# A third buffer for the adaLN filler's weight tiles, each asked for two steps ahead, in a two-layer hybrid diffusion step

## The chip, the core and the metric

The kernel runs on one core of one Trainium2 chip, as one program. The metric is the device time of one execution in microseconds; of several runs the median counts. Engines are named as in the profile: PE (TensorE, matrix products; its weight loads are PEld), DVE (VectorE), ACT (ScalarE), POOL (GpSimd) and SP (SyncE, which here does nothing but issue DMAs). Each engine works through its own list of instructions in the order in which it stands there; semaphores make one engine wait for another or for a DMA.

## The reference, cut to what matters

Two layers (`DEPTH = 2`, `D_MODEL = 2048`) over 128 context tokens and 512 latent tokens, in float32. In each layer a condition vector, one for the context tokens (`c_ctx`) and one for the latent ones (`c`), gives shift, scale and gate:

```python
def adaln(cvec, w, b):
    m = jax.nn.silu(cvec) @ w + b          # w: 2048 x 6144 per layer
    return jnp.split(m, 3, axis=-1)

def layer_step(x, cvec, p, rope, attend, s0_f, s0_b):
    ...
    shift, scale, gate = adaln(cvec, w_ada, b_ada)
    h = rms_norm(x, norm_g) * (1.0 + scale) + shift
    aq, ak, av, ag, bq, bff, bfb, bi, bg, cu, cv, cg = split_proj(h @ w_in)
    ...                                    # windowed attention, HGRN2 recurrence, gated MLP
    y = jnp.concatenate([a_out, b_out, c_out], axis=-1) @ w_out
    return x + gate * y, k, v, s_f, s_b
```

Latent attention works in blocks of 128 queries; a query sees the keys at most 128 positions away and all 128 cached context keys. So the block before and the block after need a triangular mask each, and the others none.

## The kernel before, in words

The 640 tokens stand on five tiles of 128 (`NT = 5`). The normed input is kept transposed, as 16 pairs (`KT = 16`, one per 128 input features) of tiles `hh` and `hl`, a float32 split in two parts for PE. Weights come from HBM as raw tiles `wr` (128x512, 256 KB), and are split by ACT into `wh` and by DVE into `wl`. A product is three matmuls: `hh` with `wh`, `hh` with `wl`, `hl` with `wh` (lines 682 to 684 with tokens on the output's partitions, 15 matmuls of 512 columns for each of the 16 `k`; line 690 the other way round). Four `wr` and three `wh`/`wl` buffers let loads and splits run ahead.

Layer 0 begins with `first_round`. It needs the scale of layer 0 before it can make any `hh`/`hl`, and gets it in six chunks of 2 or 4 `k`: for a chunk it loads that part of `w_ada` (raw tiles, also called `wa` in the profile, or `mg` where they are large), multiplies it on PE (line 249) with the condition vectors, which stand padded in the tile `pad`, and DVE writes the result to `gs` (lines 296 and 297). Then `scaled_h` makes `hh` on ACT (line 396) and `hl` on DVE (line 397) for each `k` of the chunk, and PE multiplies them with the key and value columns and with the first 128 columns of `cu`. The matmuls of one chunk run while the next chunk's scale is computed. x comes in six loads (`const_xT`), the weights of this round as `wr` or `ev`. `second_round` (query columns) gets the shift in the same way, and `bias_rows` multiplies it, in a second `pad` tile, with the weights already used and adds it to what was computed; only then are both `pad` tiles free.

The other columns of `w_ada` (gate of layer 0; shift, scale and gate of layer 1) aren't needed soon. They are the **filler**: `ada_gen` yields step by step through 16 blocks of 512 columns, and `fill()`, called after each weight group of the main path, takes 0.85, 0.5 or 1.25 steps on the average. A step loads one tile `wa` of 128x512 (256 KB, line 305) and DVE adds it, times a scalar, to the accumulator `aacc`, once for each condition vector (line 309 for the first tile of a block, line 311 for the 15 others). At a block's end PE sums `aacc` over its partitions (lines 317 and 328). There is one `aacc`, so a block's first step waits for the end of the block before. The filler's tiles come from the pool `arp`, which has two buffers; the two `pad` tiles come from the same pool.

All this is written in one order, and a scheduler then sets the order of each engine's list, by priorities, its own estimate of times and the buffers that are free. What is written under `hi()` goes ahead of the rest: the loads of weights and of the filler's tiles, and the whole start of layer 0. At most eight DMAs that SP issued are in flight: each takes one of eight semaphores in turn and waits until the DMA that had it has landed.

Of the kernel before, what the change touches and what calls it, by code (L numbers as in the profile page):

```python
# [18 lines left out]
P = 128  # L19
# [23 lines left out]
def host_consts():  # L43
    c = {}
    grid_w, theta, hd, n = 64, 10000.0, 128, 512
    row = np.repeat(np.arange(n // grid_w), grid_w).astype(np.float32)
    col = np.tile(np.arange(grid_w), n // grid_w).astype(np.float32)
    half = hd // 2
    freq = (np.float32(theta) ** (-np.arange(0, half, 2, dtype=np.float32) / np.float32(half))).astype(np.float32)
    ang = np.stack([row[:, None] * freq, col[:, None] * freq], axis=1).astype(np.float32)  # L50
    cs, sn = np.cos(ang), np.sin(ang)
    c["rope"] = np.ascontiguousarray(
        np.stack([cs, sn]).reshape(2, 4, P, hd // 2).transpose(2, 0, 1, 3)
    ).astype(np.float32)
    q = np.arange(P)[:, None]
    k = np.arange(P)[None, :]
    prev = np.where(k >= q, 0.0, NEG).astype(np.float32)
    nxt = np.where(k <= q, 0.0, NEG).astype(np.float32)
    z = np.zeros((P, P), np.float32)
    c["mask"] = np.concatenate([prev, z, nxt, z, prev, z, z, nxt], axis=1)  # L60
    misc = np.zeros((P, 256), np.float32)
    misc[:, 0:128] = np.eye(P)
    misc[:, 192:217] = 1.0
    misc[:, 192:217:5] = 0.0
    dneg = np.zeros((5, 4), np.float32)
    for i in range(4):
        dneg[i, i + 1:] = NEG
    misc[:, 224:244] = dneg.reshape(-1)
    for cd in range(2):
        misc[cd::32, 248 + cd] = 1.0  # L70
    c["misc"] = misc
    c["tri"] = np.stack([q <= k, q >= k], axis=1).astype(np.float32)
    return c


class Net:
# [7 lines left out]
    def pools(self):  # L84
        tc, ctx = self.tc, self.ctx
        ec = ctx.enter_context
        self.cst = ec(tc.tile_pool(name="cst", bufs=1))
        self.sml = ec(tc.tile_pool(name="sml", bufs=3))
        self.hp = ec(tc.tile_pool(name="hp", bufs=KT))
        self.mgp = ec(tc.tile_pool(name="mgp", bufs=5))  # L90
        self.wrp = ec(tc.tile_pool(name="wrp", bufs=4))
        self.whp = ec(tc.tile_pool(name="whp", bufs=3))
        self.arp = ec(tc.tile_pool(name="arp", bufs=2))
        self.evp = ec(tc.tile_pool(name="evp", bufs=5))
        self.gp = ec(tc.tile_pool(name="gp", bufs=7))
        self.pm = ec(tc.tile_pool(name="pm", bufs=5, space=PSUM))
        self.psd = ec(tc.tile_pool(name="psd", bufs=3, space=PSUM))
        self.dr = ec(tc.tile_pool(name="dr", bufs=1, space=DRAM))
# [35 lines left out]
    def setup(self):  # L134
        nc, I, C = self.nc, self.I, self.C
        cst = self.cst
        nc.scalar.preload_act_table_set("natural_log_exp_and_others")
        CR = self.g(128)
        nc.sync.dma_start(CR[0:16], I["c_ctx"].rearrange("(a p) -> a p", p=P))
        nc.sync.dma_start(CR[16:32], I["c"][0].rearrange("(a p) -> a p", p=P))  # L140
        misc = cst.tile([P, 256], F32, name="misc")
        nc.scalar.dma_start(misc, C["misc"])
        self.ident = misc[:, 0:128]
        self.m25 = misc[:, 192:217]
        self.dneg = misc[:, 224:244]
# [34 lines left out]
    def setup2(self):  # L180
        nc, I, C = self.nc, self.I, self.C
        cst = self.cst
        R = self.g(128)
        nc.scalar.dma_start(R[0:32], I["b_ada"][1, 0:4096].rearrange("(a p) -> a p", p=P))
        nc.scalar.dma_start(R[32:48], I["hgrn_lb"].rearrange("l d (h p) -> (l d h) p", p=P))
        nc.scalar.dma_start(R[48:50], I["hgrn_norm_g"])
        b = self.bank()
        nc.tensor.transpose(b[:, 0:50], R[0:50, :], self.ident[0:50, 0:50])
        nc.vector.tensor_copy(self.cols[:, 64:114], b[:, 0:50])
        l0, l1 = self.cols[:, 96:104], self.cols[:, 104:112]  # L190
        lt = self.g(64).rearrange("p (a b) -> p a b", a=8)
        mx, e0, e1, sm_, p0, p1 = (lt[:, i] for i in range(6))
        nc.vector.tensor_tensor(mx, l0, l1, op=ALU.max)
        nc.vector.tensor_tensor(e0, l0, mx, op=ALU.subtract)
        nc.vector.tensor_tensor(e1, l1, mx, op=ALU.subtract)
        nc.scalar.activation(lt[:, 1:3], lt[:, 1:3], AF.Exp)
        nc.vector.tensor_tensor(sm_, e0, e1, op=ALU.add)
        nc.vector.reciprocal(sm_, sm_)
        nc.vector.tensor_tensor(p0, e0, sm_, op=ALU.mult)
        nc.vector.tensor_tensor(p1, e1, sm_, op=ALU.mult)  # L200
        self.lb = cst.tile([P, 2, 8], F32, name="lb")
        self.oml = cst.tile([P, 2, 8], F32, name="oml")
        nc.vector.tensor_tensor(self.lb[:, 0], p0, p0, op=ALU.subtract)
        nc.vector.tensor_tensor(self.lb[:, 1], p0, p1, op=ALU.add)
        nc.vector.tensor_tensor(self.lb[:, 1], self.lb[:, 1], p0, op=ALU.subtract)
        nc.vector.tensor_scalar(self.oml, self.lb, -1.0, 1.0, op0=ALU.mult, op1=ALU.add)
        self.rope = cst.tile([P, 2, 4, 64], F32, name="rope")
        nc.scalar.dma_start(self.rope, C["rope"])
        self.scan_f = cst.tile([P, T], BF16, name="scan")
        nc.vector.memset(self.scan_f, 1.0)  # L210
        nc.vector.memset(self.scan_f[:, 0:T:32], 0.0)
        self.m8 = cst.tile([P, 2, P], U8, name="m8")
        mf = self.g(256)
        nc.scalar.dma_start(mf, C["tri"].rearrange("p d k -> p (d k)"))
        nc.vector.tensor_copy(self.m8.rearrange("p d k -> p (d k)"), mf)
        self.mask = cst.tile([P, 8 * P], BF16, name="mask")
        for i in range(2):
            mf = self.g(512)
            nc.scalar.dma_start(mf, C["mask"][:, 512 * i:512 * i + 512])
            nc.vector.tensor_copy(self.mask[:, 512 * i:512 * i + 512], mf)  # L220
        self.att = [cst.tile([P, P], F32, name=f"att{d}") for d in range(2)]
        self.tp = [cst.tile([P, 5, 5], F32, name=f"tp{i}") for i in range(2)]
        for d in range(2):
            nc.gpsimd.memset(self.tp[d], 0.0)
            nc.gpsimd.memset(self.att[d], 0.0)
        self.snk = cst.tile([P, 2, 8], F32, name="snk")
        self.nsnk = cst.tile([P, 2, 8], F32, name="nsnk")
        nc.scalar.dma_start(self.snk, I["attn_sink"].partition_broadcast(P))
        nc.vector.tensor_scalar(self.nsnk, self.snk, -1.0, None, op0=ALU.mult)
        self.gd = [self.dr.tile([2, D], F32, name=f"gd{l}", tag=f"gd{l}") for l in range(DEPTH)]  # L230
        self.cud = [self.dr.tile([P, T], F32, name=f"cud{h}", tag=f"cud{h}") for h in range(4)]
        self.x1 = [self.dr.tile([P, D], F32, name=f"x1_{t}", tag=f"x1_{t}") for t in range(NT)]
# [63 lines left out]
            nc.vector.scalar_tensor_tensor(gs, ps, 1.0, col(48 + 32 * l), op0=ALU.add, op1=ALU.add)  # L296
            nc.vector.tensor_tensor(gs, gs, col(16 * l), op=ALU.mult)

    def ada_steps(self, l, blk):
        nc = self.nc  # L300
        acc = self.sml.tile([P, 2, 512], F32, tag="aacc", name=self.nm("aacc"), bufs=1)
        for k in range(KT):
            with self.hi():
                r = self.arp.tile([P, 512], F32, tag="ar", name=self.nm("wa"))
                nc.sync.dma_start(r, self.I["w_ada"][l, k * P:(k + 1) * P, 512 * blk:512 * blk + 512])
            for cd in range(2):
                sc = self.s2[:, k, cd:cd + 1]
                if k == 0:
# [22 lines left out]
        yield  # L331

    def ada_gen(self, items):
        for it in items:
            yield from self.ada_steps(*it)

    def fill(self):
        self.credit += self.fill_rate
# [371 lines left out]
    def colmajor(self, W, c0):  # L710
        ps = [self.mbank() for _ in range(2)]
        for k4 in range(0, KT, 4):
# [7 lines left out]


    KPOS = {1: 3, 2: 4, 3: 0, 4: 1}
    WIN = {1: (((2, 1, 3),), 5, (0, 1, 2)),
# [3 lines left out]

    def kblk(self, gi, part):
        return self.kT[:, gi, part]
# [165 lines left out]
    def attn(self, l, gi, t):  # L895
# [11 lines left out]
        if t > 0:  # L907
# [9 lines left out]
            for h in range(4):  # L917
# [1 line left out]
                hs = slice(h * P, h * P + P)  # L919
                o = 0  # L920
                for p0, ds, pn in pieces:
                    ks = slice(p0, p0 + ds * pn, ds)
                    so = s[:, o * P:(o + pn) * P].rearrange("p (b k) -> p b k", k=P)
                    for i, (x, y) in enumerate(((qh, kh), (qh, kl), (ql, kh))):
                        nc.tensor.matmul(so, lhsT=x[:, hs], rhs=y[:, ks], start=i == 0, stop=i == 2,  # L925
# [525 lines left out]
```

## Time and profile before

| what | value |
|---|---|
| median of 3 runs | 2282.91 us (2281.86 to 2283.32) |
| profiled execution, its own time | 2287.63 us |
| its span, first to last instruction | 2285.8 us |
| PE busy | 2242.6 us, 98% |
| DVE busy | 1381.1 us, 60% |
| ACT busy | 943.9 us, 41% |
| DMA | 299.03 MB, mean 131 GB/s |

The first two lines differ by 4.7 us: the profiled execution is a run of its own. Its time is 1.8 us longer than the span of its instructions. In the profile's rows, `out<-in` names what an instruction writes and reads, without buffer numbers; x and a number is a count; in a timeline the first number is the start in us, the second the busy time, and the bracket at the end the engine's idle time just before, with what ended it. PE's records overlap, since its ends are modelled: the distance from start to start is what a matmul really takes. A `q` behind an engine's name means its sequencer, which issues the DMA.

### The profile page before, as it was taken

What the parts mean: (1) busy time and instruction counts of PE and PEld (TensorE: products, weight loads), DVE (VectorE), ACT (ScalarE), POOL (GpSimd) and SP (SyncE); (2) the same over time, 40 slices, a digit from 0 to 9 for tenths busy, and PEclk for the clock granted to TensorE, in tenths of its full rate; (3) what the DMA queues carried; (4) which work ended last, traced back from release to release, by engine and by line L of the source; (5) the groups of instructions that cost most, each with busy time, mean ns of one, the idle gap of its engine ahead of it and who ended that gap; (6) DMA issues with size and microseconds to landing.
All of it is one profiled execution on the core that took longest, in us unless ns stands there. A gap on an engine that the chain in (4) does not pass through costs nothing.

```text
span 2285.8 us, 35095 instructions
## 1 busy us (share of the span) xinstructions
PE 2242.6 (98%) x13259; PEld 1945.6 (85%) x13259; DVE 1381.1 (60%) x2666; ACT 943.9 (41%) x2306; POOL 0.7 (0%) x8
## 2 busy tenths in 40 slices
PE   7999999999999999999989999999999999999999
PEld 4766778999999998978877887799999999898887
DVE  4457967748577575776668555844846644264332
ACT  3423355445464562422223345543635545233111
POOL 0000000000000000000000000000000000000000
PEclk9999999999999999999999999999999999999999
DMA  9776533324334254465553321422423322326332
GB/s 354 243 258 209 171 95 117 117 78 145 103 114 133 83 154 129 144 224 182 177 181 94 101 61 48 131 60 82 140 76 103 111 69 82 94 70 205 113 106 79
DMA packets 265550, 299.03 MB, mean 131 GB/s; under 512 B 16771, under 2 KB 166165, under 8 KB 263845
## 3 DMA queue, kind: packets, MB, share of 16 engines
q1 hardware_dynamic: 252656, 270.09, 37.9%
q10 hardware_dynamic: 12724, 26.71, 3.7%
q8 instruction: 104, 1.70, 0.3%
q14 instruction: 66, 0.53, 0.1%
HBM read 281.69 MB, written 15.04 MB: 130 GB/s over the span
## 4 chain that ended last, share of the span: by engine, by line
PE 87%; DVE 6%; DMA 5%; ACT 1%; issue 1%; ACTq 0%; SPq 0%; DVEq 0%
PE m L690 36%; PE m L682 12%; PE m L684 12%; PE m L683 12%; DMA wa<-in_w_ada_dram 4%; DVE aacc L311 2%; PE s L249 2%; PE s L925 2%; PE s L971 1%; PE s L1138 1%; DVE wl L671 1%; PE s L983 1%; PE s L690 1%; PE s L984 1%; PE s L1153 1%
## 5 line engine op out<-in xcount | busy, mean ns | idle before, releaser
L671 DVE TENSOR_TENSOR wl<-wr,wh 128x512 fp32r<-128x512 f32 (+1 forms) x535 | 366.5, 687 | 547.5 <-ACT wh L670 546.5
L670 ACT ACTIVATE wh<-wr 128x512 fp32r<-128x512 f32 (+1 forms) x535 | 335.9, 629 | 870.6 <-PE m L684 501.7
L683 PE MATMUL m<-wl,hh 128*128 128x512 f32 x1440 | 568.1, 395 | 5.9 <-DVE wl L671 5.7
L682 PE MATMUL m<-wh,hh 128*128 128x512 f32 x1440 | 571.0, 397 | 1.6 <-ACT hh L396 1.5
L684 PE MATMUL m<-wh,hl 128*128 128x512 f32 x1440 | 566.1, 393 | 0.0
L690 PE MATMUL m<-hh,wh 128*128 128x384 f32 x2016 | 479.1, 317 | 0.2 <-DVE ev L1189 0.2
L690 PE MATMUL m<-hh,wl 128*128 128x384 f32 x2016 | 468.1, 311 | 0.0
L690 PE MATMUL m<-hl,wh 128*128 128x384 f32 x2016 | 467.3, 311 | 0.0
L311 DVE SCALAR_TENSOR_TENSOR aacc<-wa,s,aacc 128x512 f32<-128x512 f32 x480 | 344.1, 746 | 84.9 <-DMA wa<-in_w_ada_dram 82.7
L682 PEld LDWEIGHTS m<-wh,hh 128*128 128x128 f32 x1440 | 271.9, 189 | 73.8 <-issue 9.8
L683 PEld LDWEIGHTS m<-wl,hh 128*128 128x128 f32 x1440 | 272.0, 189 | 65.7 <-DVE wl L671 9.6
L690 PEld LDWEIGHTS m<-hh,wh 128*128 128x128 f32 x2016 | 310.8, 189 | 14.7 <-issue 9.3
L684 PEld LDWEIGHTS m<-wh,hl 128*128 128x128 f32 x1440 | 271.8, 189 | 58.5 <-issue 2.4
L690 PEld LDWEIGHTS m<-hh,wl 128*128 128x128 f32 x2016 | 311.5, 189 | 2.0 <-issue 1.8
L690 PEld LDWEIGHTS m<-hl,wh 128*128 128x128 f32 x2016 | 311.2, 189 | 2.0 <-issue 1.4
L1124 ACT ACTIVATE mg<-ev,Dt 128x32 f32<-128x32 f32 x480 | 113.3, 309 | 10.3 <-PE s L1138 10.1
L955 ACT ACTIVATE g<-g,st,qs 128x384 f32<-128x384 f32 (+1 forms) x64 | 48.1, 752 | 31.6 <-DVE st L951 31.6
L975 DVE TENSOR_TENSOR g<-s,g 128x512 fp32r<-128x512 f32 x56 | 38.6, 690 | 36.3 <-ACT g L974 29.2
L971 PE MATMUL s<-misc,g 128*128 128x128 f32 x240 | 45.6, 284 | 5.9 <-ACT g L960 5.1
L960 ACT ACTIVATE g<-g,st 128x384 f32<-128x384 f32 (+2 forms) x80 | 43.9, 605 | 13.3 <-DVE st L958 13.3
L925 PE MATMUL s<-kT,g 128*128 128x256 f32 (+1 forms) x288 | 47.3, 305 | 0.0
L971 PEld LDWEIGHTS s<-misc,g 128*128 128x128 f32 x240 | 29.6, 142 | 20.1 <-ACT g L960 12.3
(278 smaller groups left out, 1832.4 us busy)
## 6 DMA issues: line engine op xcount, KB each, us to landing
wr<-in_w_in_dram SPq DMA_DIRECT2D x406, 256.0 KB, 2.9
wa<-in_w_ada_dram SPq DMA_DIRECT2D x296, 256.0 KB, 2.9
wr<-in_w_out_dram SPq DMA_DIRECT2D x128, 256.0 KB, 3.0
wa<-in_w_ada_dram SPq DMA_DIRECT2D x16, 1024.0 KB, 7.0
wa<-in_w_in_dram SPq DMA_DIRECT2D x9, 1024.0 KB, 6.4
mg<-in_w_ada_dram SPq DMA_DIRECT2D x4, 1280.0 KB
x<-mg SPq DMA_DIRECT2D x20, 256.0 KB, 2.6
mg<-x ACTq DMA_DIRECT2D x5, 1024.0 KB, 6.1
```

The source lines that it names most:

```text
L249: return self.nc.tensor.matmul(acc[32 * q:32 * q + 32, 0:n], lhsT=lhs[:, kk, :], rhs=rhs, start=kk < 4, stop=kk >= 12, skip_group_check=True)
L311: nc.vector.scalar_tensor_tensor(acc[:, cd], r, sc, acc[:, cd], op0=ALU.mult, op1=ALU.add)
L670: nc.scalar.activation(wh, raw, AF.Copy)
L671: nc.vector.tensor_tensor(wl, raw, wh.bitcast(F32), op=ALU.subtract)
L682: nc.tensor.matmul(ps, lhsT=hh, rhs=wh[:, 0], start=k == 0, stop=False)
L683: nc.tensor.matmul(ps, lhsT=hh, rhs=wl[:, 0], start=False, stop=False)
L684: nc.tensor.matmul(ps, lhsT=hl, rhs=wh[:, 0], start=False, stop=k == KT - 1)
L690: self.nc.tensor.matmul(ps[hf][:, 0:n], lhsT=w[:, a], rhs=h[:, o:o + n], start=k == 0 and i == 0, stop=k == KT - 1 and i == 2)
L925: nc.tensor.matmul(so, lhsT=x[:, hs], rhs=y[:, ks], start=i == 0, stop=i == 2, skip_group_check=True)
L955: nc.scalar.activation(dst[h], src[h], AF.Exp, bias=nmx[:, h:h + 1], scale=rq[:, h:h + 1], accum_out=den[:, h:h + 1])
L971: nc.tensor.transpose(pb[:, h * P:(h + 1) * P], dst[h][:, kb * P:(kb + 1) * P], self.ident)
L1124: nc.scalar.activation(blk[:, 4 * i + q], e[:, q], AF.Copy, scale=dd[:, i, c:c + 1])
```

## The change

Three things. The pool `arp` gets a third buffer. The load of a filler tile goes into a function of its own, `ada_load`, which takes the next tile from a list that runs over all blocks; `ada_gen` calls it twice before the first step, and each step calls it once more before it takes its own tile from the front of the queue `ahead`. To make room in SBUF, the mask tile shrinks from eight blocks of 128 columns to four, and a constant tile from 256 columns to 192; the table `WIN`, which says for each query block which key blocks are read in which order and where its mask begins, changes with it.

```diff
-    c["mask"] = np.concatenate([prev, z, nxt, z, prev, z, z, nxt], axis=1)
-    misc = np.zeros((P, 256), np.float32)
+    c["mask"] = np.concatenate([prev, z, z, nxt], axis=1)
+    misc = np.zeros((P, 192), np.float32)
...
-        self.arp = ec(tc.tile_pool(name="arp", bufs=2))
+        self.arp = ec(tc.tile_pool(name="arp", bufs=3))
...
-        self.mask = cst.tile([P, 8 * P], BF16, name="mask")
-        for i in range(2):
-            mf = self.g(512)
-            nc.scalar.dma_start(mf, C["mask"][:, 512 * i:512 * i + 512])
-            nc.vector.tensor_copy(self.mask[:, 512 * i:512 * i + 512], mf)
+        self.mask = cst.tile([P, 4 * P], BF16, name="mask")
+        mf = self.g(512)
+        nc.scalar.dma_start(mf, C["mask"])
+        nc.vector.tensor_copy(self.mask, mf)
...
-    def ada_steps(self, l, blk):
+    def ada_load(self, tiles):
+
+        at = next(tiles, None)
+        if at is None:
+            return
+        l, blk, k = at
+        with self.hi():
+            r = self.arp.tile([P, 512], F32, tag="ar", name=self.nm("wa"))
+            self.nc.sync.dma_start(r, self.I["w_ada"][l, k * P:(k + 1) * P, 512 * blk:512 * blk + 512])
+        self.ahead.append(r)
+
+    def ada_steps(self, l, blk, tiles):
         nc = self.nc
         acc = self.sml.tile([P, 2, 512], F32, tag="aacc", name=self.nm("aacc"), bufs=1)
         for k in range(KT):
-            with self.hi():
-                r = self.arp.tile([P, 512], F32, tag="ar", name=self.nm("wa"))
-                nc.sync.dma_start(r, self.I["w_ada"][l, k * P:(k + 1) * P, 512 * blk:512 * blk + 512])
+            self.ada_load(tiles)
+            r = self.ahead.pop(0)
...
     def ada_gen(self, items):
-        for it in items:
-            yield from self.ada_steps(*it)
+        tiles = iter([(l, blk, k) for l, blk in items for k in range(KT)])
+        self.ahead = []
+        for _ in range(2):
+            self.ada_load(tiles)
+        for l, blk in items:
+            yield from self.ada_steps(l, blk, tiles)
...
-           2: (((3, 1, 2), (0, 2, 2)), 0, (1, 2, 3, 0)),
-           3: (((4, -2, 2), (0, 1, 2)), 4, (2, 0, 3, 4)),
+           2: (((3, 1, 2), (2, -2, 2)), 0, (1, 2, 0, 3)),
+           3: (((4, -2, 2), (0, 1, 2)), 0, (2, 0, 3, 4)),
```

The diff doesn't show where the scheduler now puts the filler's instructions. Line numbers grow: 305 becomes 306, 309 and 311 become 318 and 320, 396 and 397 become 409 and 410, 427 becomes 440, 438 becomes 451, 671 becomes 684.

On SP, in the first round, where the third piece of x is loaded (`mg65`; `wa52` is the last scale tile for k = 4 to 7, `ev66` and on are weights). Before:

```order
L438 DMA wa52_226<-in_w_ada_dram 128x512
L427 DMA mg65_320<-const_xT_dram 128x2560
L461 DMA ev66_322<-in_w_in_dram 128x512
L461 DMA ev67_324<-in_w_in_dram 128x512
L461 DMA ev68_326<-in_w_in_dram 128x512
L461 DMA ev69_328<-in_w_in_dram 128x512
L662 DMA wr70_330<-in_w_in_dram 128x4x128
```

In the changed kernel (`wa316`, `wa317`, `wa319` and `wa325` are the filler's first four tiles):

```order
L451 DMA wa52_226<-in_w_ada_dram 128x512
L306 DMA wa316_1719<-in_w_ada_dram 128x512
L440 DMA mg65_320<-const_xT_dram 128x2560
L306 DMA wa317_1721<-in_w_ada_dram 128x512
L474 DMA ev66_322<-in_w_in_dram 128x512
L474 DMA ev67_324<-in_w_in_dram 128x512
L474 DMA ev68_326<-in_w_in_dram 128x512
L474 DMA ev69_328<-in_w_in_dram 128x512
L306 DMA wa319_1724<-in_w_ada_dram 128x512
L675 DMA wr70_330<-in_w_in_dram 128x4x128
L451 DMA mg72_333<-in_w_ada_dram 128x5x512
L306 DMA wa325_1762<-in_w_ada_dram 128x512
```

The filler's loads, which before came only after the second round, now stand between those of the first round. Each of them but the first waits on SP for the steps on the filler's tile before it; the fifth tile, `wa331`, follows four scale tiles later, the sixth, `wa337`, another four later, and all sixteen tiles of block 0 stand before the end of the first round or just behind it.

On DVE, at the same place: from the first split weight of k = 2 (`wl85`) to `hl87`, which belongs to k = 2 as well; `gs_150<-s40` is the scale of the chunk with k = 2 and 3. Before:

```order
L671 TENSOR_TENSOR wl85_358<-wr38_199,wh84_357 128x512
L671 TENSOR_TENSOR wl89_391<-wr39_201,wh88_390 128x512
L296 SCALAR_TENSOR_TENSOR gs_150<-s40_203,cols_146 128x4
L297 TENSOR_TENSOR gs_150<-gs_150,cols_146 128x4
L671 TENSOR_TENSOR wl96_432<-g15_122,wh95_431 128x256
L397 SCALAR_TENSOR_TENSOR hl87_362<-mg12_116,gs_150,hh86_361 128x128
```

In the changed kernel, where just ahead of the first of these rows stands the pair of steps on `wa316`:

```order
L684 TENSOR_TENSOR wl85_358<-wr38_199,wh84_357 128x512
L320 SCALAR_TENSOR_TENSOR aacc318_1723<-wa317_1721,s2_137,aacc318_1723 128x512 x2
L684 TENSOR_TENSOR wl89_391<-wr39_201,wh88_390 128x512
L320 SCALAR_TENSOR_TENSOR aacc318_1723<-wa319_1724,s2_137,aacc318_1723 128x512
L295 SCALAR_TENSOR_TENSOR gs_150<-s40_203,cols_146 128x4
L320 SCALAR_TENSOR_TENSOR aacc318_1723<-wa319_1724,s2_137,aacc318_1723 128x512
L296 TENSOR_TENSOR gs_150<-gs_150,cols_146 128x4
L684 TENSOR_TENSOR wl96_432<-g15_122,wh95_431 128x256
L320 SCALAR_TENSOR_TENSOR aacc318_1723<-wa325_1762,s2_137,aacc318_1723 128x512 x2
L320 SCALAR_TENSOR_TENSOR aacc318_1723<-wa331_1800,s2_137,aacc318_1723 128x512 x2
L320 SCALAR_TENSOR_TENSOR aacc318_1723<-wa337_1838,s2_137,aacc318_1723 128x512
L410 SCALAR_TENSOR_TENSOR hl87_362<-mg12_116,gs_150,hh86_361 128x128
```

The steps on five and a half filler tiles now stand ahead of `hl87`, and those on two and a half ahead of the first `gs` of this chunk. Of the ten later tiles of block 0, two (`wa372` and `wa401`) put one of their two steps between the two instructions on `gs` of a later chunk; the other steps stand between weights and sums of squares, and the first step on `wa401` stands right ahead of such a `gs`, one weight behind the steps on `wa383`, the tile before it.

On SP in the output projection of layer 0, where the filler is in its ninth block (`wr` are tiles of `w_out`; counted over all blocks, `wa1696` of before and `wa1692` of the change are the 131st filler tile, `wa1700` and `wa1693` the 132nd). Before:

```order
L662 DMA wr1714_10082<-in_w_out_dram 128x512
L305 DMA wa1696_9974<-in_w_ada_dram 128x512
L662 DMA wr1718_10107<-in_w_out_dram 128x512
L662 DMA wr1722_10132<-in_w_out_dram 128x512
L305 DMA wa1700_9999<-in_w_ada_dram 128x512
```

In the changed kernel:

```order
L675 DMA wr1715_10083<-in_w_out_dram 128x512
L306 DMA wa1693_9950<-in_w_ada_dram 128x512
L675 DMA wr1719_10108<-in_w_out_dram 128x512
L675 DMA wr1723_10133<-in_w_out_dram 128x512
L306 DMA wa1697_9975<-in_w_ada_dram 128x512
```

At the same weights the filler is one tile further: the place of the 131st tile is now that of the 132nd, and the 131st went out some dozen loads earlier. On DVE the steps are packed more densely there: the 16 steps of the ninth block stand among 12 weights before and among 10 after, those of the tenth among 9 before and 7 after.

More of the change, by code (lines that the diff above doesn't have):

```diff
@@ L59, in host_consts @@
     z = np.zeros((P, P), np.float32)
-    c["mask"] = np.concatenate([prev, z, nxt, z, prev, z, z, nxt], axis=1)
-    misc = np.zeros((P, 256), np.float32)
+    c["mask"] = np.concatenate([prev, z, z, nxt], axis=1)
+    misc = np.zeros((P, 192), np.float32)
     misc[:, 0:128] = np.eye(P)
-    misc[:, 192:217] = 1.0
-    misc[:, 192:217:5] = 0.0
+    misc[:, 128:153] = 1.0
+    misc[:, 128:153:5] = 0.0
     dneg = np.zeros((5, 4), np.float32)
@@ L67, in host_consts @@
         dneg[i, i + 1:] = NEG
-    misc[:, 224:244] = dneg.reshape(-1)
+    misc[:, 160:180] = dneg.reshape(-1)
     for cd in range(2):
-        misc[cd::32, 248 + cd] = 1.0
+        misc[cd::32, 184 + cd] = 1.0
     c["misc"] = misc
@@ L140, in setup @@
         nc.sync.dma_start(CR[16:32], I["c"][0].rearrange("(a p) -> a p", p=P))
-        misc = cst.tile([P, 256], F32, name="misc")
+        misc = cst.tile([P, 192], F32, name="misc")
         nc.scalar.dma_start(misc, C["misc"])
         self.ident = misc[:, 0:128]
-        self.m25 = misc[:, 192:217]
-        self.dneg = misc[:, 224:244]
-        self.sel = misc[:, 248:250]
+        self.m25 = misc[:, 128:153]
+        self.dneg = misc[:, 160:180]
+        self.sel = misc[:, 184:186]
         R = self.g(128)
@@ L722 @@
     KPOS = {1: 3, 2: 4, 3: 0, 4: 1}
-    WIN = {1: (((2, 1, 3),), 5, (0, 1, 2)),
[3 rows of a table removed]
+    WIN = {1: (((2, 1, 3),), 1, (0, 1, 2)),
[3 rows of a table added]
     def kblk(self, gi, part):
@@ L921, in attn @@
                 for p0, ds, pn in pieces:
-                    ks = slice(p0, p0 + ds * pn, ds)
+                    ks = slice(p0, p0 + ds * pn if p0 + ds * pn >= 0 else None, ds)
                     so = s[:, o * P:(o + pn) * P].rearrange("p (b k) -> p b k", k=P)
```

2 rows, old and new, of the table WIN are left out of this document.

## The prediction

> **What bounds the kernel now.** I read the page first: busy shares, slices, costliest groups.
>
> ```profile
> span 2285.8 us, 35095 instructions
> PE 2242.6 (98%) x13259; PEld 1945.6 (85%) x13259; DVE 1381.1 (60%) x2666; ACT 943.9 (41%) x2306; POOL 0.7 (0%) x8
> ...
> L311 DVE SCALAR_TENSOR_TENSOR aacc<-wa,s,aacc 128x512 f32<-128x512 f32 x480 | 344.1, 746 | 84.9 <-DMA wa<-in_w_ada_dram 82.7
> ```
>
> TensorE (PE) is the bound: 98% of the span. VectorE (DVE) is idle for 82.7 us because the filler's tile (`wa`) has not landed, but this is idle time of an engine that is busy for 60%. It is worth only what PE loses by it. So the second view is the table of waits for PE:
>
> ```profile
> PE m L683 <- DVE wl L671: 5.7, 5, 2.5
> PE s L638 <- issue: 5.3, 1, 5.3
> PE s L971 <- ACT g L960: 5.1, 5, 2.1
> PE s L643 <- DVE g L647: 2.5, 1, 2.5
> PE s L1138 <- DVE mg L1109: 2.4, 1, 2.4
> ...
> PE s L1103 <- ACT g L1099: 1.4, 1, 1.4
> ```
>
> The timeline of DVE shows what stands ahead of two of these; the others look alike:
>
> ```profile
> 348.78 0.75 DVE L311 SCALAR_TENSOR_TENSOR aacc<-wa,s,aacc 128x512 f32<-128x512 f32 x1 [2.07 <-DMA wa<-in_w_ada_dram]
> ...
> 991.27 0.75 DVE L311 SCALAR_TENSOR_TENSOR aacc<-wa,s,aacc 128x512 f32<-128x512 f32 x1 [3.81 <-DMA wa<-in_w_ada_dram]
> ```
>
> Lines 683, 971, 1138 and 1103 are those where DVE or ScalarE (ACT) came late behind a filler step; lines 638 and 643 are the border between the layers, where the filler has no part. So all that better filler loads can return is 5.7 + 5.1 + 2.4 + 1.4 = 14.6 us, 0.6% of the span. The third view is the table by stages, for the start:
>
> ```profile
> 18.70:57.00 38.30, 37.74 (x208) 25.14 (x209) 19.03 (x35) 17.72 (x33) 0.00 (x0) 1.00 1.04 387
> 57.00:114.00 57.00, 57.00 (x336) 43.25 (x338) 25.01 (x48) 24.73 (x49) 0.00 (x0) 1.00 0.71 244
> ```
>
> (busy us of PE, weight load, DVE, ACT, POOL; then clock, share of the DMA engines, GB/s.) From 18.7 to 57 us PE and the DMA engines are both full, and DVE is half idle. That is where the change puts its first sixteen tiles.
>
> **The change, part by part.** *The mask.* One load of 256 KB and one of two casts go:
>
> ```profile
> L220 DVE CAST mask<-g x2: 421/424/428, 200.5 to 201.6; 128x512 bf16<-128x512 f32 x2
> ```
>
> 0.42 us of DVE at 200 us, beside a busy PE: 0 (between -0.4 and 0). The attention blocks only change places; the same matmuls run.
>
> *The third buffer at the start.* The pool `arp` lends its first two buffers to `pad` tiles until the second round and the bias rows are over, so before, the filler could not load until then. The third is free from the beginning, and the order shows what the scheduler does with it: block 0 of the filler runs through this single buffer during the first round. With one buffer, a load waits for both steps on the tile before, on SP's queue, and the steps wait for the load, on DVE's queue; whatever stands behind either waits too. DVE works in the order written, and the steps on five and a half tiles stand ahead of `hl87`, the third operand of k = 2. So I follow that chain with the rows of before. When the loads go out:
>
> ```profile
> 30.76 0.43 SPq L427 DMA_DIRECT2D mg<-const_xT_dram  x1
> 31.65 2.37 SPq L461 DMA_DIRECT2D ev<-in_w_in_dram  x4
> ```
>
> How long they take there, in the DMA view of 28 to 42 us:
>
> ```profile
> DMA packets 2763, 5.43 MB, mean 388 GB/s; under 512 B 246, under 2 KB 758, under 8 KB 2634
> ...
> wa<-in_w_ada_dram SPq DMA_DIRECT2D x10, 256.0 KB, 8.3
> mg<-const_xT_dram SPq DMA_DIRECT2D x1, 1280.0 KB, 8.0
> ```
>
> And how long with nothing ahead of them (whole run), with the step that starts a block (the others take 746 ns):
>
> ```profile
> wa<-in_w_ada_dram SPq DMA_DIRECT2D x296, 256.0 KB, 2.9
> ```
>
> ```profile
> L309 DVE TENSOR_SCALAR aacc<-wa,s x32: 469/478/486, 186.2 to 1749.0; 128x512 f32<-128x512 f32 x32
> ```
>
> DVE and PE at this place before:
>
> ```profile
> 21.43 0.83 DVE L480 TENSOR_TENSOR g<-g,g 128x640 f32<-128x640 f32 x1 [0.47 <-ACT g L478]
> ...
> 31.71 0.16 DVE L296 SCALAR_TENSOR_TENSOR gs<-s,cols 128x4 f32<-128x4 f32 x1 [1.09 <-PE s L261]
> 31.91 0.16 DVE L297 TENSOR_TENSOR gs<-gs,cols 128x4 f32<-128x4 f32 x1
> ...
> 33.19 0.35 DVE L397 SCALAR_TENSOR_TENSOR hl<-mg,gs,hh 128x128 fp32r<-128x128 f32 x1
> ```
>
> ```profile
> 33.16 0.50 PE L682 MATMUL m<-wh,hh 128*128 128x512 f32 x1 [0.56 <-ACT hh L396]
> 33.50 0.40 PE L683 MATMUL m<-wl,hh 128*128 128x512 f32 x1
> 33.73 0.40 PE L684 MATMUL m<-wh,hl 128*128 128x512 f32 x1
> ```
>
> A 256 KB tile is 0.68 us at 388 GB/s, the 1280 KB x tile 3.4. The first tile, wa316, takes the x tile's place in SP's queue, at 30.8; the x tile landed at 38.8, so the smaller one lands at 38.8 - 4 x 0.68 = 36.0. DVE has nothing else to do in its order from 22.3 on: it stands until 36.0. Then round by round (land; steps done; next load out 0.1 later; it lands 2.9 after, or when the queue ahead of it is through, if that is later):
> - wa316: 36.0, two steps of 0.48, 37.0.
> - wa317: out 37.1, behind the x tile (through at 39.5): lands 40.2; two steps, 41.6.
> - wa319: out 41.7, lands 44.6; first step 45.3, `gs`, second step and `gs` again: 46.4 where 32.1 stood before; k = 2 can begin at 47.5 with its first two matmuls, and stops at the third, for `hl87`.
> - wa325: out 46.2, behind a 256 KB and a 1280 KB load: lands 49.4; steps, 50.8.
> - wa331: out 50.9, lands 53.8; 55.2.
> - wa337: out 55.3, lands 58.2; first step 58.9; then `hl87` at 59.3.
>
> So the third matmul of k = 2 starts at 59.4 and not at 33.73: **+25.7 us**, and PE has nothing else in its order meanwhile. Six round trips can't be much shorter than 4.2 us each; if a load takes 2.4 it is +23, if the two round trips through a full queue take a microsecond more it is +28. Later PE is the bound again and never gives it back.
>
> [...]
>
> *PE after standing still.* The only other long stop, between the layers, is followed by slow matmuls:
>
> ```profile
> 1197.50 1.05 PE L638 MATMUL s<-misc,mg 128*128 128x128 f32 x4 [5.27 <-issue]
> ...
> 1206.56 0.63 PE L682 MATMUL m<-wh,hh 128*128 128x512 f32 x1
> 1206.99 0.63 PE L683 MATMUL m<-wl,hh 128*128 128x512 f32 x1
> ```
>
> 0.43 from start to start, against 0.23 at 33.50. PE now stands for some 14 and then 11 us; I take ten matmuls that are 0.20 slower, **+2.0** (0 to 4).
>
> *The other ten early tiles* (wa342 on). After k = 2 PE is 26 us late and the loads of later chunks were issued meanwhile, so these tiles mostly land before DVE, half idle in the row of 57 to 114 us, comes to them. Two of them put a step of 0.75 between the two `gs` instructions on which PE waits: 1.5. One (wa401) is asked for only after the step on wa383, which stands one weight ahead of it:
>
> ```profile
> 87.27 0.69 DVE L671 TENSOR_TENSOR wl<-ev,wh 128x512 fp32r<-128x512 f32 x1 [3.51 <-ACT wh L670]
> 89.55 0.16 DVE L296 SCALAR_TENSOR_TENSOR gs<-s,cols 128x4 f32<-128x4 f32 x1 [1.59 <-PE s L261]
> ```
>
> wa383's steps end about 86.9 (in times of before), wa401 lands at 89.9 and its step ends at 90.6: `gs` is 1.0 late. Sum **+2.5**; from 0, if all hide, to 10 x 4.4 = 44, if each is a round trip of its own. I stay near 0, since DVE's row shows the room.
>
> *Two steps ahead, afterwards.* From block 1 on all three buffers serve the filler. While a tile loads (2.9 + 0.1), DVE has the steps on one other tile to do now, 1.5 us, and on two others then, 3.0; and each load stands about one tile earlier in SP's queue. Most waits of DVE for `wa` go. But the order packs the steps more densely between the weights (two per weight: 2 x 1.49 + 0.69 = 3.7 us, where PE needs 15 x 0.23 = 3.4 for a row-major one), so weights are late next. Of 14.6 I take **-10** (0 to -14.6).
>
> Sum: 25.7 + 2.0 + 2.5 - 10 = +20.2. The profiled execution took 2287.63 us, so it would be 2307.8; it lies 4.7 above the median of 2282.91, and the forecast for the median is **2303 us**.
>
> **Rivals.**
> - *Faster.* The start hides the sixteen tiles and the full 14.6 comes: 2268. For it: DVE is half idle there and steps taken early are not due later. Against it: it would need wa316 landed when DVE comes to it at 22.3, and it is asked for at 30.8. It decides from a start cost under 10 us. [...]
> - *Only bytes.* The engines' waits cost nothing and each tile only its own 0.68 us of the full queue: 16 x 0.68 = 10.9, less the gain of 10: 2284. For it: DVE's idle half. Against it: both queues are worked in order.
> - *The third buffer does nothing after the start*, since SP's queue holds each load behind weights that wait for their own slots: +30.2, 2313.
> - *More round trips.* Half of the other ten tiles stop DVE at 4.4 each, +22 more: 2325.
>
> **How the numbers follow.** The forecast has 0.60 (its own range 2294 to 2313: 23 to 28 for the chain, 0 to 4 for the slow PE, 4 to 14 of gain); third buffer idle 0.14; more round trips 0.16; faster 0.05; only bytes 0.05. A measurement tells 0.2% (4.6 us) from no change. "Faster" alone lies below that, "only bytes" inside it with a little of its spread on the slow side, the rest above: 0.05 faster, 0.04 same, 0.91 slower. Range 2290 to 2320: it leaves out "faster", "only bytes" and more than half of "more round trips".
>
> **What the profile after would show.** Between 18.7 and 57 us PE is busy for about 15 us and not 37.7; DVE's timeline has a row on `aacc` with some 14 us of idle time before it, from a `wa` that lands near 36, and five more at 3 us each; the third matmul of k = 2 starts near 59. DVE's waits for `wa` after 300 us fall well below 80 us, and the 14.6 of PE's waits to about 5. I would be wrong if DVE passed these steps without a stop, if the start cost under 15 us, or if PE made up time in a stage that has none to give.

## The result, and the profile after

The changed kernel takes 2298.99 us (median of four runs, 2296.78 to 2300.57), the kernel before 2283.11 (2281.86 to 2283.86): ratio 1.0064, with a 95% interval of 1.0052 to 1.0076. It is slower by 15.9 us; the forecast was 20.2 slower, 2303 us. The profiled execution of the changed kernel took 2296.78 us, 2.2 below its median.

The page of the changed kernel, the lines that answer to those shown of before:

```profile
span 2295.0 us, 35054 instructions
PE 2237.1 (97%) x13259; PEld 1944.3 (85%) x13259; DVE 1378.1 (60%) x2665; ACT 945.1 (41%) x2306; POOL 0.7 (0%) x8
...
L320 DVE SCALAR_TENSOR_TENSOR aacc<-wa,s,aacc 128x512 f32<-128x512 f32 x480 | 336.7, 743 | 41.0 <-DMA wa<-in_w_ada_dram 40.4
```

Read alone, this is a success: DVE waits 40.4 us for the filler's tiles where it waited 82.7, with the same work. The table by stages (columns as before: busy us of PE, weight load, DVE, ACT, POOL; clock, DMA share, GB/s) shows what it is worth:

```profile
18.70:57.00 38.30, 14.40 (x80) 10.01 (x78) 9.86 (x18) 7.33 (x14) 0.00 (x0) 0.73 0.91 323
57.00:114.00 57.00, 51.27 (x274) 34.82 (x275) 32.97 (x58) 20.42 (x37) 0.00 (x0) 0.91 0.82 274
```

From 18.7 to 57 us PE was busy for 37.74 us before and is for 14.40 now. The DMA engines are less busy there too (0.91, 1.04 before): this stage has not become a matter of bytes. The table of waits of PE over the whole run (what waits, on what; us in total, times, longest):

```profile
PE m L695 <- ACT hh L409: 16.3, 3, 14.9
PE m L697 <- DVE hl L410: 14.8, 1, 14.8
...
PE s L651 <- issue: 4.0, 1, 4.0
PE m L696 <- DVE wl L684: 3.4, 1, 3.4
...
PE s L1151 <- ACT mg L1137: 0.4, 1, 0.4
PE s L984 <- ACT g L973: 0.3, 1, 0.3
```

Two new stops of 14.8 us at the start; and of the 14.6 us that better loads could return, 3.4 + 0.4 + 0.3 = 4.1 are left. DVE's timeline at the start shows the chain behind the two stops (start, busy us; the bracket is the idle time before):

```profile
36.36 0.88 DVE L318 TENSOR_SCALAR aacc<-wa,s 128x512 f32<-128x512 f32 x2 [14.71 <-DMA wa<-in_w_ada_dram]
37.16 0.68 DVE L684 TENSOR_TENSOR wl<-wr,wh 128x512 fp32r<-128x512 f32 x1
40.21 1.41 DVE L320 SCALAR_TENSOR_TENSOR aacc<-wa,s,aacc 128x512 f32<-128x512 f32 x2 [2.37 <-DMA wa<-in_w_ada_dram]
...
44.69 0.75 DVE L320 SCALAR_TENSOR_TENSOR aacc<-wa,s,aacc 128x512 f32<-128x512 f32 x1 [2.46 <-DMA wa<-in_w_ada_dram]
...
46.09 0.15 DVE L296 TENSOR_TENSOR gs<-gs,cols 128x4 f32<-128x4 f32 x1
...
52.21 1.41 DVE L320 SCALAR_TENSOR_TENSOR aacc<-wa,s,aacc 128x512 f32<-128x512 f32 x2 [5.63 <-DMA wa<-in_w_ada_dram]
56.42 1.41 DVE L320 SCALAR_TENSOR_TENSOR aacc<-wa,s,aacc 128x512 f32<-128x512 f32 x2 [2.79 <-DMA wa<-in_w_ada_dram]
61.66 0.75 DVE L320 SCALAR_TENSOR_TENSOR aacc<-wa,s,aacc 128x512 f32<-128x512 f32 x1 [3.83 <-DMA wa<-in_w_ada_dram]
62.33 1.01 DVE L410 SCALAR_TENSOR_TENSOR hl<-mg,gs,hh 128x128 fp32r<-128x128 f32 x2
```

Six landings, six waits: DVE works for some 1.4 us on a tile and then stands until the next one lands. `hl87` comes at 62.33.

### The profile page after: what moved, and what is told of

The parts are those of the page before. It is cut to its first block, busy times and chain, and to the rows that moved or that the text cites. A ratio compares the mean times of both kernels' runs of the same rounds, so it can differ in the third digit from the quotient of the medians.

```text
span 2295.0 us, 35054 instructions
## 1 busy us (share of the span) xinstructions
PE 2237.1 (97%) x13259; PEld 1944.3 (85%) x13259; DVE 1378.1 (60%) x2665; ACT 945.1 (41%) x2306; POOL 0.7 (0%) x8
## 4 chain that ended last, share of the span: by engine, by line
PE 89%; DVE 3%; DMA 1%; ACT 1%; issue 1%; ACTq 0%; DVEq 0%
PE m L703 39%; PE m L695 13%; PE m L697 12%; PE m L696 12%; PE s L938 2%; PE s L984 1%; PE s L1151 1%; PE s L248 1%; DMA wa<-in_w_ada_dram 1%; DVE wl L684 1%; PE s L997 1%; PE s L996 1%; PE s L1166 1%; PE s L1116 1%; PE s L337 1%; DVE aacc L320 1%
## 5 line engine op out<-in xcount | busy, mean ns | idle before, releaser
L697 PE MATMUL m<-wh,hl 128*128 128x512 f32 x1440 | 567.6, 394 | 14.8 <-DVE hl L410 14.8
L320 DVE SCALAR_TENSOR_TENSOR aacc<-wa,s,aacc 128x512 f32<-128x512 f32 x480 | 336.7, 743 | 41.0 <-DMA wa<-in_w_ada_dram 40.4
L697 PEld LDWEIGHTS m<-wh,hl 128*128 128x128 f32 x1440 | 272.0, 189 | 72.3 <-DVE hl L410 15.9
L987 ACT ACTIVATE g<-s 128x512 fp32r<-128x512 f32 x56 | 32.5, 596 | 37.6 <-PE s L984 29.3
L942 DVE CUSTOM_DVE_ANT_0 g<-s,mask 128x384 f32<-128x384 f32 (+1 forms) x64 | 38.0, 621 | 15.2 <-PE s L938 15.0
```

What stands on the lines that cost most here:

```text
L320: nc.vector.scalar_tensor_tensor(acc[:, cd], r, sc, acc[:, cd], op0=ALU.mult, op1=ALU.add)
L697: nc.tensor.matmul(ps, lhsT=hl, rhs=wh[:, 0], start=False, stop=k == KT - 1)
```

## The experiments

The question is whether the loss is that chain, what in the chain costs (DVE's time, bytes, or one of the two lists), and which part of the change makes the gain behind it. Where a lag is given, it is the start of the same matmul (the n-th of those with `wh` and `hh`) in two traces, one minus the other; it is as good as the profiled execution it comes from, 2 to 4 us. The medians decide. For comparison with the kernel before, each group of runs had runs of it on the same chip, with medians of 2283.55 (hold to two_ahead1), 2283.99 (dose1 to mask_only), 2282.85 (pool_steps) and 2284.18 (stops).

### hold: the filler kept out of the start

```diff
+        self.hold = self.padded()            # a third pad tile, zeros, from arp
-            nc.vector.tensor_copy(b, self.rows_cols(acc, rows, P)[:, 0])
+            nc.vector.tensor_tensor(b, self.rows_cols(acc, rows, P)[:, 0], self.hold[:, 0, 0:2], op=ALU.add)
```

> The changed kernel with the third buffer lent to a third tile of zeros until the bias rows are over, as the two pad tiles are, so that the filler cannot load before the second round (one addition of zeros is added, 0.1 us of DVE). Theory A (the loss is the chain of round trips through one free buffer at the start; afterwards the change gains): no loss at the start, the gain stays: 2283.1 - 10 to - 22 = 2261 to 2273, with PE busy for 37 of the 38.3 us from 18.7 to 57 us. Rival B (the loss comes later, from loads that stand ahead of weights in SP's queue): still above 2290. Rival C (what PE wins back after 360 us is only the late start made up, no gain of the change): 2283, the same as before.

Measured: 2268.04 us (2266.55 to 2270.47), ratio to before 0.9933, interval 0.9921 to 0.9946. PE in the first stage, and what is left of its waits in the whole run:

```profile
18.70:57.00 38.30, 37.74 (x209) 25.10 (x208) 18.81 (x34) 17.11 (x32) 0.00 (x0) 1.00 1.05 388
```

```profile
PE s L652 <- issue: 4.0, 1, 4.0
PE m L697 <- DVE wl L685: 3.8, 2, 3.5
PE s L657 <- DVE g L661: 1.7, 1, 1.7
...
PE s L985 <- ACT g L974: 1.4, 2, 1.1
...
PE s L657 <- ACT mg L643: 0.7, 1, 0.7
```

So the change is the sum of two things that can be had apart: a start that costs 2298.99 - 2268.04 = **31.0 us**, and a gain of 2283.55 - 2268.04 = **15.5 us** (12 to 18 by the interval). Theory A holds; B and C fall. This kernel beats both.

### hold_noahead and two_ahead1: the buffer, or asking ahead?

hold_noahead is hold without the two loads ahead of the first step; two_ahead1 has two buffers and one load ahead.

```diff
-        for _ in range(2):
-            self.ada_load(tiles)
```

> As hold, but each tile is asked for in its own step, as before the change: the third buffer without asking ahead. If the buffer alone makes the gain, since the scheduler hoists a load anyway as soon as a buffer is free: within 3 us of hold. If asking two steps ahead makes it: 2283, the same as before.

```diff
-        self.arp = ec(tc.tile_pool(name="arp", bufs=3))
+        self.arp = ec(tc.tile_pool(name="arp", bufs=2))
...
-        for _ in range(2):
-            self.ada_load(tiles)
+        self.ada_load(tiles)
```

> The smaller mask, two buffers as before, each tile asked for one step ahead. With two buffers the start is as before the change (no filler load before the second round). If the buffer is what counts: 2283 within 0.2%. If asking ahead counts by itself: 2268 to 2278.

Measured: hold_noahead 2267.82 us (2267.09 to 2268.35), ratio 0.9931 (0.9919 to 0.9944), the same as hold. two_ahead1 2281.20 (2279.40 to 2283.93), ratio 0.9991 (0.9982 to 1.0000). The buffer makes the gain. Asking ahead in the program adds nothing: the time is the same whichever step the load is written in, as it would be if the scheduler moves a load forward as far as a free buffer lets it. (The 2.3 us of two_ahead1 are looked at under mask_only.)

### third_noahead: what pulls the tiles into the start

The edit of hold_noahead in the changed kernel, without the held tile.

> The changed kernel with each tile asked for in its own step; the third buffer is free from the beginning. Theory A: the scheduler puts block 0 through the single buffer at the start just the same, and the time is that of the change, 2295 to 2303, with PE busy for about 15 of the 38.3 us from 18.7 to 57 us. Rival D (asking ahead is what pulls the loads into the start): 2283 or less.

Measured: 2297.76 us (2294.77 to 2298.81), ratio 1.0057 (1.0043 to 1.0071); PE is busy for 14.63 us of the first stage. Here too it is the free buffer and not the asking. Theory A holds, D falls.

### mask_only: the smaller mask alone

Two buffers and no loads ahead.

> The smaller mask and constant tile alone: two buffers, each tile asked for in its own step. No instruction on the path changes: 2283.5 within 0.1%. If the order of the attention blocks or the one load and cast that are gone count: 2280 to 2282, as two_ahead1 with its 2281.2 may suggest.

Measured: 2281.65 us (2277.90 to 2284.92, 11 runs), ratio 0.9991 (0.9982 to 1.0000). That is -2.3 us, with 0 at the end of the interval; two_ahead1 shows the same -2.3 with the same mask. The third buffer's own part is then 2267.82 - 2281.65 = -13.8. The traces show a place for the 2.3. On line 971 of before, in the attention (982 in mask_only, 983 in two_ahead1), PE waits for ACT for 5.1 us, at most 2.1 at a time, and for 2.6 and 3.0 in these two, at most 0.8 and 1.4. The stop of 2.43 us at 740.5 is one of 1.95 in both, with the granted clock at 1.00 around it (737 to 752 and 735 to 752) where before had 0.77. So a part of the 14.6 us that the prediction put down to the filler's loads goes with the mask: 12.0 are left on the same lines in mask_only. Which part of the smaller mask does it (the other order of the key blocks, or the load that is gone) isn't shown.

### dose1 and dose3: how many tiles go through the one buffer

```diff
+        self.a3p = ec(tc.tile_pool(name="a3p", bufs=1))
-        self.arp = ec(tc.tile_pool(name="arp", bufs=3))
+        self.arp = ec(tc.tile_pool(name="arp", bufs=2))
...
+            i, self.nth = self.nth, self.nth + 1
+            third = i < 3 or i % 3 == 2          # dose1: i < 1 or i % 3 == 0
-            r = self.arp.tile([P, 512], F32, tag="ar", name=self.nm("wa"))
+            r = (self.a3p if third else self.arp).tile([P, 512], F32, tag="ar", name=self.nm("wa"))
```

> The third buffer is a pool of its own; of the filler's tiles only the first, wa316, may use it at the start, the second waits for the two pad tiles, and after that every third tile uses it. The tile after the first three that goes through this buffer is still loaded early, but no step waits for it there. The chain of round trips: DVE stops until 36.4, steps to 37.3, the two instructions on gs right behind, 5.6 later than 31.71 before the change; so 2268 + 5.6, with 1 for slow matmuls: 2273 to 2276. A cost spread evenly over the 16 early tiles (bytes, queue places): 31 / 16 = 1.9 for one: 2270.

> As dose1, with the first three tiles through the third buffer at the start. The chain of round trips: the third tile's second step ends at 46.1 in the profile of the change, hl87 follows 1.3 later at 47.4 where 33.2 stood before: +14.2, and 1 to 2 for slow matmuls: 2283 to 2285. Spread evenly over 16 tiles: 2268 + 3 x 1.9 = 2274.

| kernel | tiles through one buffer | lag to hold at the 40th matmul | median - 2268.04 |
|---|---|---|---|
| dose1, 2278.60 (2275.79 to 2283.33) | 1 | 8.5 | 10.6 |
| dose3, 2287.40 (2284.92 to 2290.61) | 3 | 16.1 | 19.4 |
| the change, 2298.99 | 16, of which six ahead of `hl87` | 31.0 | 31.0 |

Ratios to before: 0.9977 (0.9968 to 0.9986) and 1.0015 (1.0006 to 1.0024). Spread evenly over 16 tiles, one tile would cost 1.9 us and three 5.8: that falls. By the lags, the first tile costs 8.5, the next two 3.8 each, the three after them 5.0 each. Both medians lie some 2.5 us above the range that was expected. DVE in dose1 shows one reason:

```profile
37.31 0.88 DVE L321 TENSOR_SCALAR aacc<-wa,s 128x512 f32<-128x512 f32 x2 [14.83 <-DMA wa<-in_w_ada_dram]
38.11 1.29 DVE L687 TENSOR_TENSOR wl<-wr,wh 128x512 fp32r<-128x512 f32 x2
39.31 0.15 DVE L296 SCALAR_TENSOR_TENSOR gs<-s,cols 128x4 f32<-128x4 f32 x1
```

Behind the waiting step two weights had queued up as well; `gs` comes at 39.31, 7.6 after 31.71, where 5.6 was expected. After 180 us PE waits for a tile of cached keys (`g<-in_cache_k_dram`) for 3.6 and 3.4 us in these two kernels, for 1.2 in hold. That does not explain the rest: in dose3 the lag goes from 16.1 at the 161st matmul to 19.7 at the 201st and is back at 16.0 at the 551st. Why the medians of both lie 2 to 3 us above the lags at the start stays open.

### tiny_steps: is it DVE's time?

```diff
+                if l == 0 and blk == 8 and k:
+                    nc.vector.scalar_tensor_tensor(acc[:, cd, 0:32], r[:, 0:32], sc, acc[:, cd, 0:32], op0=ALU.mult, op1=ALU.add)
```

> The changed kernel with the steps of block 0 (all but its first tile) cut to 32 of 512 columns, which leaves out most of the gate's first 512 columns of layer 0; the loads stay whole and in their places. The chain of round trips: each of five trips loses some 1.2 of 4.4 us, but one of them waits for the queue either way: hl87 at 56 to 58 instead of 62.3, and about 1 more later: 2299 - 5 to - 8 = 2291 to 2294. If the loss is DVE's time for the steps (16 x 1.49 = 24 us moved into the start): 2268 to 2276.

Measured: 2297.21 us (2294.47 to 2297.83), ratio 1.0056 (1.0043 to 1.0069). That DVE's time is the cost falls: the sum for it was 2268 to 2276. The chain's own sum, 2291 to 2294, was missed by 3 us, since the round trips did not get as much shorter as expected (`hl87` comes at 59.24):

```profile
39.78 0.41 DVE L318 SCALAR_TENSOR_TENSOR aacc<-wa,s,aacc 128x32 f32<-128x32 f32 x2 [2.37 <-DMA wa<-in_w_ada_dram]
...
45.08 0.41 DVE L318 SCALAR_TENSOR_TENSOR aacc<-wa,s,aacc 128x32 f32<-128x32 f32 x2 [4.28 <-DMA wa<-in_w_ada_dram]
...
58.91 0.42 DVE L318 SCALAR_TENSOR_TENSOR aacc<-wa,s,aacc 128x32 f32<-128x32 f32 x2 [3.95 <-DMA wa<-in_w_ada_dram]
```

The steps take 0.41 where they took 1.41, but DVE then waits longer: 18.6 us in its five waits for tiles from the second tile to `hl87`, against 17.1 in the changed kernel. The third tile, asked for at 40.23, lands at 45.08; in the changed kernel, asked for at 41.65, at 44.69. Here asking 1.4 us earlier did not make the tile land earlier. Other loads stood ahead of it in both kernels, and the DMA engines were busy for 82% of the wait in one and 89% in the other; which of the loads held it up isn't shown.

### pool_steps: DVE's list and SP's list apart

```diff
+                if l == 0 and blk == 8:
+                    nc.gpsimd.tensor_copy(acc[:, cd], r)
```

> The changed kernel with the steps of block 0 done by POOL, as plain copies of the tile (so the gate's first 512 columns of layer 0 are not computed); SP's list begins as in the changed kernel, through its first seven filler tiles, and DVE's has no step of block 0. This parts the two lists. If DVE's list alone makes the loss at the start: at most 2271, since DVE now waits for nothing. If SP's list alone makes it (loads of scale tiles and weights behind filler loads that wait for the one buffer): 2295 or more. If both, as the prediction has it: k = 2 begins as before the change, and the chunk from k = 4 on comes late, because its last scale tile goes out after wa337, near 58 where hold has it near 47: 2268 + 8 to 16, so 2276 to 2284, with PE's wait on the third chunk and not on k = 2.

Measured: 2284.46 us (2280.32 to 2289.72), ratio 1.0005 (0.9995 to 1.0016), 16.4 above hold: the third case, just above its upper end. POOL takes DVE's place in the chain, PE's waits between 30 and 115 us follow, and then PE where the longer ones end:

```profile
36.31 1.16 POOL L318 COPY aacc<-wa 128x512 f32<-128x512 f32 x2 [35.12 <-DMA wa<-in_w_ada_dram]
40.53 1.18 POOL L318 COPY aacc<-wa 128x512 f32<-128x512 f32 x2 [3.06 <-DMA wa<-in_w_ada_dram]
45.55 1.17 POOL L318 COPY aacc<-wa 128x512 f32<-128x512 f32 x2 [3.84 <-DMA wa<-in_w_ada_dram]
```

```profile
PE m L697 <- ACT wh L685: 6.1, 1, 6.1
PE s L260 <- ACT g L253: 4.3, 1, 4.3
```

```profile
72.24 1.06 PE L260 MATMUL s<-misc,g 128*128 128x2 f32 x8 [4.33 <-ACT g L253]
...
95.19 0.79 PE L697 MATMUL m<-wh,hh 128*128 128x512 f32 x1 [6.10 <-ACT wh L685]
```

k = 2 starts at 32.1, as before. SP's list alone costs 15.2 us (lag at the 60th matmul): the chunk from k = 8 gets its scale late, at 72, and a weight comes late at 95. I had expected one chunk earlier; the scale tiles that stand behind `wa325` to `wa337` belong to that later chunk. In the changed kernel this second delay does not add to the first: there PE comes to that chunk 31 us later anyway. So DVE's list sets the loss, and SP's alone, with POOL in DVE's place, makes half of it. (The two waits are 10.4 us and the lag 15.2: PE again loses more than it waits, which the last experiment looks at.)

### stops: what a stop of PE is worth

```diff
-        nc.vector.tensor_tensor(wl, raw, wh.bitcast(F32), op=ALU.subtract)
+        self.nsplit = getattr(self, "nsplit", 0) + self.late
+        for _ in range({22: 13, 38: 15, 54: 20}.get(self.nsplit, 1)):
+            nc.vector.tensor_tensor(wl, raw, wh.bitcast(F32), op=ALU.subtract)
```

`nsplit` counts the weights from layer 1's output projection on (`late` is 1 there and 0 before); the lines that set `late` are left out here.

> The kernel hold with three stops of PE put into the last three column blocks of layer 1's output projection, where hold has PE busy without a gap and at clock 1.00 from 2100 to 2264 us: at one weight of each block DVE writes the same wl 13, 15 and 20 times instead of once (0.6 us apart; the result does not change). wl is finished about 6 us before its use, so PE should stop for about 1, 2 and 5 us, 8 to 9 in all. If a stop costs its own length: the end comes later by the sum of the three waits, near 2277. If the matmuls after a stop are slower too, as before the change behind the stop of 2.43 us at 740.5 (clock 0.77 in the 15 us from 737): 1.5 to 2.5 more for each stop, so the end is later by 1.5 to 2 times the waits, 2281 to 2284.

Measured: 2291.59 us (2288.87 to 2292.88), ratio to before 1.0032 (1.0019 to 1.0045), 23.6 above hold. The waits of PE there, and its timeline at the first:

```profile
PE m L699 <- DVE wl L687: 16.1, 3, 8.3
```

```profile
2119.60 0.50 PE L699 MATMUL m<-wl,hh 128*128 128x512 f32 x1 [3.18 <-DVE wl L687]
2119.94 0.39 PE L700 MATMUL m<-wh,hl 128*128 128x512 f32 x1
2120.17 0.40 PE L699 MATMUL m<-wl,hh 128*128 128x512 f32 x1
...
2121.25 0.63 PE L699 MATMUL m<-wl,hh 128*128 128x512 f32 x1
2121.67 0.63 PE L700 MATMUL m<-wh,hl 128*128 128x512 f32 x1
...
2124.23 0.44 PE L698 MATMUL m<-wh,hh 128*128 128x512 f32 x1
2124.51 0.40 PE L699 MATMUL m<-wl,hh 128*128 128x512 f32 x1
```

The waits were longer than planned (3.2, 4.6 and 8.3 us), since `wl` was ready less early than I took it to be. Against hold, the matmuls behind the three stops are late by 5.1, 7.4 and 10.7 us: each stop costs its length and **1.9 to 2.8 us more**, about the same for a short and for a long one. The granted clock is 0.79 in the 8 us from 2119, 0.77 in the 15 us from 2175 and 0.66 in the 15 us from 2240; it is 1.00 in hold from 2100 to 2264. Together 23.2 for 16.1: the first reading falls, and the second holds for the amount of each stop (1.5 to 2.5 more). Its factor of 1.5 to 2 was for shorter stops; here it is 1.44, and since the extra does not grow with the length, it is no factor for stops of another length.

## Why the prediction came out as it did

The direction, the place and the mechanism were right. The loss at the start came out near its sum because errors cancelled; the gain afterwards was taken too small, and that makes the distance from 20.2 to 15.9.

- **The chain, +25.7.** The third matmul of k = 2 starts at 62.73 in the changed kernel, at 33.45 in hold and at 33.73 before: 29.0 to 29.3. The first half came as worked out (36.36 for 36.0, 40.21 for 40.2, 44.69 for 44.6, the second `gs` at 46.09 for 46.4). The mis-sized step is the landing of wa325, at 52.2 and not at 49.4; another 0.7 is in the trip of wa337, which lands 9.5 behind wa325 where 8.8 was reckoned. What SP issues there, and what the DMA view of the changed kernel shows between the landings of the third tile and of wa325:

```profile
46.20 0.34 SPq L306 DMA_DIRECT2D wa<-in_w_ada_dram  x1
46.64 1.86 SPq L451 DMA_DIRECT2D wa<-in_w_ada_dram  x4
```

```profile
DMA packets 1281, 2.41 MB, mean 322 GB/s; under 512 B 83, under 2 KB 109, under 8 KB 1281
```

  I had counted three loads, 1.84 MB, at 388 GB/s: 4.7 us. It was 2.41 MB at 322 GB/s: 7.5 us. So at least 0.57 MB came from loads issued behind wa325 (the row of four), which I had given no share of the DMA engines before it landed. And the rate that I took from a stage in which the DMA engines were full (share 1.05 from 28 to 42 us before) did not hold here, where the share is 0.93. The bound of 28 gave the two trips through a full queue a microsecond more each, which was too little for wa325.
- **PE after standing still, +2.0.** Lag to hold of 31.0 at the 20th matmul less 29.3: 1.7. The matmuls after the first stop were slow too (0.59 us to the next start at 46.73, where hold has 0.33 at 32.89), but only two of them ran before the second stop.
- **The other ten early tiles, +2.5.** From 31.0 at the 20th matmul to 32.1 at the 80th: 1.1. They hide.
- **The start in sum, +30.2.** 31.0 by the medians of the change and hold. Three terms off by +3.5, -0.3 and -1.4 leave 1.8 by the lags, 0.8 by the medians: that the sum came so near is luck.
- **Two steps ahead, -10 of at most 14.6.** 15.5 (12 to 18), or 13 to 14 without the 2.3 of the smaller mask. This term, too small by 3 to 5.5 us, is the one that takes the forecast off. The waits of PE on the lines named in the prediction went from 14.6 before to 5.2 in hold (3.8 + 1.4): 9.4 less, as forecast. What was wrong is that each wait was counted at its length: I had charged slow matmuls after the stops at the start, and forgot that a stop that goes takes its slow matmuls with it. The granted clock (third number from the right) shows them, first before, then in hold:

```profile
346.00:360.00 14.00, 11.90 (x69) 10.69 (x67) 8.89 (x17) 5.67 (x12) 0.00 (x0) 0.88 0.51 157
430.00:445.00 15.00, 13.37 (x86) 11.69 (x85) 11.91 (x22) 7.91 (x14) 0.00 (x0) 1.00 0.46 136
737.00:752.00 15.00, 12.57 (x85) 10.45 (x84) 8.01 (x20) 9.53 (x38) 0.00 (x0) 0.77 0.37 109
1005.00:1030.00 25.00, 22.40 (x98) 17.97 (x98) 20.24 (x34) 6.59 (x15) 0.00 (x0) 0.93 0.66 220
1190.00:1212.00 22.00, 14.13 (x64) 11.13 (x63) 20.57 (x43) 14.93 (x36) 0.00 (x0) 0.84 0.31 106
```

```profile
970.00:995.00 25.00, 21.46 (x82) 17.19 (x81) 19.53 (x31) 3.79 (x6) 0.00 (x0) 0.86 0.70 226
1175.00:1200.00 25.00, 18.58 (x88) 14.87 (x87) 23.49 (x49) 16.21 (x39) 0.00 (x0) 0.80 0.28 95
```

  Place by place, by the lag of before to hold (their two profiled executions end 17.2 apart):

| us, in times of before | stops of PE, before and hold, us | granted clock there (in the stretches above, where a row shows one), before and hold | lag grows by, us |
|---|---|---|---|
| 345 to 368 | 2.1 and none | 0.88 and 1.00 | 3.6 |
| 554 to 572 | 1.4 and none | 1.00 and 1.00 | 1.6 |
| 726 to 761 | 2.4 and none | 0.77 and 1.00 | 5.3 |
| 979 to 1024, output projection of layer 0 | 5.1 and 3.5 | 0.93 and 0.86 | 1.6 |
| 1146 to 1217, border between the layers | 8.4 and 6.4 | 0.84 and 0.80 | 3.0 |

  The two stops with slow matmuls behind them, 4.5 us long, were worth 8.9; the one without was worth its length. In the last two rows hold has shorter stops but a lower clock, and only the growth of the lag is measured: what else makes these 4.6 us isn't shown. Taken together, all of PE's waits after the start went from 25.6 to 14.2 and the lower clock (1 less the clock, times the stretch, summed over the rows) cost at most 10.4 us before and 8.5 in hold. That makes some 13 of the 17.2; the rest stays open.
- **The name of that part** was wrong as well: the third buffer gives it, and asking two steps ahead gives nothing.
- **The mask, 0.** -2.3, at the edge of what was measured. "The same matmuls run" was right, but PE waits less in the attention (line 971, under mask_only).

Of the rivals, *Only bytes* falls by the doses, *The third buffer does nothing after the start* by hold, *More round trips* by the ten tiles that hide. *Faster* falls by the start. Its price of 2268 is the time of the kernel whose start is left alone, but by luck: it took all 14.6 us of waits as gone, and in hold 5.2 of them are still there.

## What to carry to other kernels

An extra buffer does not only deepen the pipeline that it is meant for: a scheduler that takes any free buffer, as this one did, uses it at the first moment it exists. If that is earlier than the other buffers come free, a prefetch turns into a chain of load, use, load, use through one slot, and everything behind it on the engine's list, urgent or not, waits for each landing. So look at where the first use of a new buffer lands in the lists, and hold the buffer back (here with one idle tile that lives as long as its neighbours) if that place is tight: a loss of 15.9 us became a gain of 15.5. And price a stop of PE, one that comes or one that goes, not at its length alone: those of 2.1 to 8.3 us cost 1.5 to 2.9 us more here, one of 1.4 us nothing more.

## What the hardware showed that I had not expected

After the stop of 3.18 us PE first ran on at full pace, 0.23 us from start to start, for about 1.3 us, and only then fell to 0.43 for 3 us. After the stops of 14.8 us the first matmul was slow already (0.59 to the next start, at 46.73 and at 62.73, with the granted clock at 0.50 from 36 to 67 us). In the kernel before, a stop of 2.10 us was followed by slow matmuls and one of 1.61 us was not (clock 0.88 and 1.00 in the rows of 346 and 430 us); nor was one of 1.95 us in mask_only (clock 1.00 from 737 to 752):

```profile
351.09 0.69 PE L971 MATMUL s<-misc,g 128*128 128x128 f32 x2 [2.10 <-ACT g L960]
...
434.70 0.44 PE L971 MATMUL s<-misc,g 128*128 128x128 f32 x2 [1.61 <-ACT g L960]
```

A 256 KB tile asked for 1.4 us earlier (40.23 for 41.65) landed 0.4 us later (45.08 for 44.69): with other loads in flight, the moment of asking said little about the moment of landing. And a load that was issued first did not have the DMA engines to itself until it landed: of the 2.41 MB that moved before wa325 was there, at least 0.57 were of loads issued behind it.
